# Last four softmax heads: values product with queries on partitions, sums divided on the copy, turns by VectorE in blocks

## The chip, the cores and the metric

The kernel runs on one core of one Trainium2 chip. The metric is the device time of one execution in microseconds; the time before is the median of three runs.

## The reference

One decoder layer on x of shape (1, 512, 2048), float32. What matters here is the dilated softmax mixer with eight heads of width 128:

```
h  = rms_norm(x, g1);  proj = h @ w_in            # all projections in one
qb, kb = rms_norm(qb), rms_norm(kb)               # per head
for (window, dilation) in ((128,1), (512,4), (2048,16)):
    logits = q @ k.T / sqrt(128) + bias[distance];  masked, causal
    o, lse = softmax(logits) @ v, log-sum-exp
out_b = sum over the three branches, weighted by softmax of their lse
x = x + concat(out_a, out_b) @ w_out              # out_a: gated linear attention, 4 heads
x = x + swiglu(rms_norm(x)) @ ...                 # w_gate, w_up, w_down
```

The kernel merges the three branches into one softmax over all 512 keys: a table holds, for each distance, the bias plus the logarithm of the number of branches in which the distance occurs.

## The kernel before

**Large products.** All five weight matrices are multiplied by a scheme with seven block products in place of eight (the names P1 to P7; `Pair` and `stream`). A step of the stream is one weight group of 256 rows by 512 columns. ScalarE casts it to a high part (`wh`, line 376), VectorE subtracts for the low part (`wl`, line 380), and sums of two weight blocks are made on VectorE too (line 294). TensorE then issues twelve matmuls of 128x512 (line 405), eight with `wh` and four with `wl`. Between the eight and the four, `p.step()` lets a piece of other work in. There are two buffers each of `wh` and `wl`.

**Other work.** The heads run as generators in the list `background`; one `yield` to the next is one piece, and a rate for each pair of weight blocks says how many pieces a step takes. The eight softmax heads come in twos: `dil_heads(h)` advances head h (lane 0) and h+1 (lane 1) in turn. Heads 0 to 3 start when the projection `vb0` is stored, heads 4 to 7 when `qb1` is. The latter run beside the pair of weight blocks that makes the output gate (28 steps, called the gate pair here). The three engines TensorE, ScalarE and VectorE and the queues follow an order that the framework's scheduler works out from the program; the order by hand in `PLAN` holds for the first pair alone.

**A softmax head.** It loads queries, keys, values and the bias table. For heads 0 to 3 (`s == 0`) the queries and keys are loaded by `load_blocks` (line 842): four DMAs per tile, one for each 32 columns, so that VectorE's transpose of 32x32 blocks (line 992) gives the full transpose. For heads 4 to 7 they are loaded by one DMA per tile (line 983) and turned by four TensorE transposes each (line 998) into a bank that ScalarE copies out, with the query gain (line 999). Then six pieces: scores of a query block (line 1007), bias and row extreme on VectorE (1010), exponential with row sum on ScalarE (1013), reciprocal (1016) and multiplication (1017) on VectorE; a piece later the turn of the weights on TensorE (1024) and their copy (1027); another piece later the product with the values, which stand as the stationary operand (1031), so that the output has the head's features on partitions, and its copy (1043). The last piece stores the head's output to `mix_d` (1047).

**After the heads.** `mix_d[4]` to `mix_d[7]` each hold two heads. The script `GATE` says at which step of the gate pair `mixed` does what: `T.g` loads the group's two halves of tokens (line 1222, two DMAs, as `kept[g, "t0"]` and `"t1"`), `A11.g`, `S3.g` and so on make sums of them (lines 1284 to 1294) and split them into high and low operands (lines 194 and 195). Groups 2 and 3 hold heads 4 to 7. The output projection (`w_out`) reads them.

All DMAs of this part are issued by SP, one after the other. A DMA whose data is not ready holds those behind it.

Of the kernel before, what the change touches and what calls it, by code (L numbers as in the profile page):

```python
# [10 lines left out]
F32 = mybir.dt.float32  # L11
F32R = mybir.dt.float32r
U32 = mybir.dt.uint32
AF = mybir.ActivationFunctionType
ALU = mybir.AluOpType
# [3 lines left out]
P = 128  # L19
S = 512  # L20
# [11 lines left out]
    13: "A11.1",  # L32
    14: "S3.1",
    16: "T.2",
    19: "A11.2",
    20: "S3.2",
    21: "2.0 S1.0",
# [1 line left out]
    23: "S1.1",  # L39
    24: "S2.0",  # L40
    25: "T.3 S2.1",
    27: "A11.3",
}
OUT = {
    0: "S3.3",
# [81 lines left out]
def block_kernel(ctx: ExitStack, tc: tile.TileContext, ins, out):  # L127
    nc = tc.nc
# [5 lines left out]
    apool = ctx.enter_context(tc.tile_pool(name="apool", bufs=28))  # L134
# [12 lines left out]
    def nm(s):  # L147
        uid[0] += 1
        return f"{s}_{uid[0]}"

    def dram(shape, name):
        return dr.tile(shape, F32, name=name, tag=name)

    def bank():
        return ps.tile([P, 512], F32, name=nm("bank"), tag="bank")

    def work(tag, shape=(P, 512), bufs=1):
        return mp.tile(list(shape), F32, name=nm(tag), tag=tag, bufs=bufs)

    def const(shape, name):  # L160
        return cp.tile(list(shape), F32, name=name, tag=name)
# [3 lines left out]
    load = nc.sync.dma_start  # L165
    store = nc.sync.dma_start

    mats = const([P, 2, P], "mats")
    ident, causal = (mats[:, i, :] for i in range(2))
# [11 lines left out]
    recent = {}  # L181
    done = set()
# [83 lines left out]
    def halves(t):  # L266
        return t.rearrange("p (b a) -> p b a", b=2)
# [377 lines left out]
    gq = const([P, 1], "gq")  # L645
# [78 lines left out]
    for g in range(4):  # L724
        for b in (2 * g, 2 * g + 1):
            if g < 2:
                t = apool.tile([P, 2, 512], F32, name=nm("xT"), tag="A")
# [57 lines left out]
    def gates():  # L785
# [30 lines left out]
        for h in range(4):  # L816
# [13 lines left out]
    proj = {n: dram([S, 512], n) for n in  # L830
            ("qa", "ka", "va0", "va1", "qb0", "kb0", "vb0", "vb1", "qb1", "kb1")}
    ong_d = [dram([2, P, 1024], f"ong_d{t}") for t in range(2)]
    mix_d = [dram([2, P, 2, 256], f"mix_d{b}") for b in range(8)]

    def head_cols(src, h, w=P):
        return src.rearrange("(t p) c -> p t c", p=P)[:, :, h * w : (h + 1) * w]

    def load_blocks(t, src, h):

        for a in range(4):  # L840
            c0 = h * P + 32 * a
            load(
                t[32 * a : 32 * a + 32, :].rearrange("i (c j) -> i c j", j=32),
                src[:, c0 : c0 + 32].rearrange("(c i) j -> i c j", i=32),
            )
# [115 lines left out]
    def dil_head(h, lane):  # L961


        s = h // 4

        def tile_(name):
            if lane == 0:
                return work("oT" if name == "o" else name)
            if name in "qk":
                return work(name + "T")  # L970
            return rpool.tile([P, 512], F32, name=nm("r"), tag="r")

        def logits(b):
            if lane == 0:
                return work("L", bufs=2)
            return tile_("L") if b % 2 else work("PT")

        qh, kh, vh = tile_("q"), tile_("k"), tile_("v").rearrange("p (t d) -> p t d", t=4)
        for dst, name in ((qh, f"qb{s}"), (kh, f"kb{s}")):
            if s == 0:  # L980
                load_blocks(dst, proj[name], h)
            else:
                load(dst.rearrange("p (t d) -> p t d", t=4), head_cols(proj[name], h % 4))
        load(vh, head_cols(proj[f"vb{s}"], h % 4))
        tb = tile_("T")
        load(tb, bass.AP(
            tensor=rep_d.tensor, offset=h * P * NB + P - 1, ap=[[NB - 1, P], [1, 512]]
        ))
        yield
        for src, g in ((qh, gq), (kh, 1.0)):  # L990
            if s == 0:
                nc.vector.transpose(src, src)
                if src is qh:
                    nc.scalar.activation(src, src, AF.Copy, scale=g)
                continue
            tp = bank()
            for t in range(4):
                nc.tensor.transpose(tp[:, t * P : (t + 1) * P], src[:, t * P : (t + 1) * P], ident)
            nc.scalar.activation(src, tp, AF.Copy, scale=g)
        yield  # L1000
        ot = tile_("o")
        lgs = {}

        def scores(b):
            n = P * (b + 1)
            lp = bank()
            nc.tensor.matmul(lp[:, :n], qh[:, b * P : (b + 1) * P], kh[:, :n], start=True, stop=True)  # L1007
            lg = lgs[b] = logits(b)
            st = work("mx", (P, 4), bufs=4)
            recent["head"] = nc.vector.tensor_tensor_reduce(  # L1010
                lg[:, :n], lp[:, :n], tb[:, 512 - n :], -1.0, 3.0e38, ALU.add, ALU.min, st[:, 0:1]
            ).ins
            nc.scalar.activation(
                lg[:, :n], lg[:, :n], AF.Exp, scale=-1.0, bias=st[:, 0:1], accum_out=st[:, 2:3]
            )
            nc.vector.reciprocal(st[:, 3:4], st[:, 2:3])
            recent["head"] = nc.vector.tensor_scalar(
                lg[:, :n], lg[:, :n], st[:, 3:4], None, op0=ALU.mult
            ).ins

        def turn(b, tp):
            n = P * (b + 1)
            for k in range(b + 1):
                nc.tensor.transpose(  # L1024
                    tp[:, k * P : (k + 1) * P], lgs[b][:, k * P : (k + 1) * P], ident
                )
            nc.scalar.copy(lgs[b][:, :n], tp[:, :n])

        def values(b, op):
            for k in range(b + 1):  # L1030
                nc.tensor.matmul(  # L1031
                    op, vh[:, k, :], lgs[b][:, k * P : (k + 1) * P], start=(k == 0), stop=(k == b)
                )

        for i in range(6):
            tp = bank() if 1 <= i <= 4 else None
            if i >= 2:
                op = tp[:, i * P : (i + 1) * P] if i < 4 else bank()[:, :P]
                values(i - 2, op)
            if tp is not None:  # L1040
                turn(i - 1, tp)
            if i >= 2:
                nc.scalar.copy(ot[:, (i - 2) * P : (i - 1) * P], op)
            if i < 4:
                scores(i)
            if i == 5:
                store(mix_d[4 + h // 2][:, :, h % 2, :].rearrange("b p n -> p b n"), halves(ot))
            yield

    def dil_heads(h):  # L1050

        lanes = [dil_head(h, 0), dil_head(h + 1, 1)]
        for _ in range(8):
            for lane in lanes:
                next(lane)
            if _ == 7:
                done.update((id(mix_d[4 + h // 2]), half) for half in range(2))
            yield
# [158 lines left out]
    def part(src, half):  # L1217
        def get(t=None):
            assert (id(src), half) in done
            if t is None:  # L1220
                t = rpool.tile([P, 2, 256], F32, name=nm("r"), tag="r")
            load(t, src[half])
            return t

        return get
# [32 lines left out]
    kept = {}  # L1258

    def scripted(pace, script):  # L1260

        k = [0]

        def go():
            pace()
            for word in script.get(k[0], "").split():
                mixed(*word.split("."))
            k[0] += 1

        return go  # L1270

    def mixed(name, g):
        g = int(g)
        tt = nc.vector.tensor_tensor
        if name == "T":
            t = apool.tile([P, 2, 2, 256], F32, name=nm("top"), tag="A")
            for i in range(2):
                kept[g, "t" + str(i)] = part(mix_d[4 + g], 1 - i)(t[:, i])
            return
        t0, t1 = kept[g, "t0"], kept[g, "t1"]  # L1280
        if name == "A11":
            opm.split(name, g, t0)
        elif name == "S3":
            tt(t1, t0, t1, op=ALU.subtract)
            opm.split(name, g, t1)
        elif name == "2":
            tt(t1, kept[g, "r1"], t1, op=ALU.subtract)
            tt(t0, t1, t0, op=ALU.add)
        elif name == "S1":
            opm.split(name, g, t0)  # L1290
        elif name == "S2":
            opm.split(name, g, t1)
        elif name == "S4":
            tt(t1, kept[g, "r0"], t1, op=ALU.subtract)
            opm.split(name, g, t1)
        else:
            opm.split(name, g, kept[g, "r0" if name == "A12" else "r1"])
# [402 lines left out]
```

## Time and profile before

| | |
|---|---|
| median of 3 runs | 1897.93 us |
| lowest, highest | 1895.16, 1898.85 us |
| the profiled execution | 1897.46 us, span 1895.70 us |
| TensorE busy | 1882.5 us, 99% |
| VectorE busy | 1691.9 us, 89% |
| ScalarE busy | 1073.1 us, 57% |
| DMA, mean | 182 GB/s |

In the rows PE is TensorE's matmul, PEld its weight load, DVE is VectorE, ACT ScalarE, SPq the queue of SyncE, which issues DMAs. L1007 is line 1007 of the kernel. `out<-in` names the program's tiles; `bank` is a PSUM bank, `wl` the low part of weights, `top` the tile of head outputs that `T.g` loads, `q`, `k`, `qT`, `kT` the queries and keys of lane 0 and lane 1.

### The profile page before, as it was taken

The numbers are of one execution on the slowest core, as the hardware profiler recorded it, in microseconds if no ns is written. First come the engines' busy times: TensorE is split into PE (matmuls) and PEld (weight loads), VectorE is DVE, ScalarE is ACT, GpSimd is POOL, SyncE is SP. The second block draws the span as 40 slices with busy tenths as digits, with TensorE's granted clock in tenths as the row PEclk, the third lists the DMA queues.
The fourth block names the chain that finished last, engine by engine and source line by source line (L and its number), as shares of the span: only waits on it lengthen the run. The fifth ranks groups of instructions, "written<-read, shape, count | busy, mean of one in ns | idle before, by whom it ended". The sixth has DMA issues, their size and how long they took to land.

```text
span 1895.7 us, 25155 instructions
## 1 busy us (share of the span) xinstructions
PE 1882.5 (99%) x8882; PEld 1636.0 (86%) x8882; DVE 1691.9 (89%) x1968; ACT 1073.1 (57%) x1583; POOL 4.5 (0%) x16
## 2 busy tenths in 40 slices
PE   9999999999999999999999999999999999999999
PEld 7888888888888888888888888888888888888887
DVE  8898898788899999888888888888889989999987
ACT  8664674577776675544544544544546546546543
POOL 0000000000000000000000000000000000000000
PEclk9999999999999999999999999999999999999999
DMA  9456545563628454465465465465466765785762
GB/s 341 161 151 237 174 154 156 173 220 107 206 101 270 146 195 143 119 185 185 130 184 178 121 196 161 123 200 155 135 200 202 207 231 184 264 279 186 241 222 67
DMA packets 271203, 345.46 MB, mean 182 GB/s; under 512 B 141908, under 2 KB 178685, under 8 KB 271078
## 3 DMA queue, kind: packets, MB, share of 16 engines
q1 hardware_dynamic: 270790, 343.73, 57.2%
q8 instruction: 69, 1.13, 0.2%
q14 instruction: 56, 0.46, 0.1%
q10 hardware_dynamic: 288, 0.14, 0.0%
HBM read 285.91 MB, written 60.32 MB: 183 GB/s over the span
## 4 chain that ended last, share of the span: by engine, by line
PE 86%; DVE 8%; DMA 3%; issue 2%; ACT 1%; SPq 0%; DVEq 0%; ACTq 0%
PE acc L405 79%; DVE wl L380 3%; PE acc L477 2%; DVE wa L294 2%; PE bank L1007 1%; PE bank L1031 1%; DMA xn_d<-oT 1%; PE bank L1024 0%; DVE AS L195 0%; PE bank L477 0%; PE bank L779 0%; DMA oT<-in_xt 0%; DMA x_d<-k 0%; DMA r<-xn_d 0%; DMA xT<-in_xt 0%
## 5 line engine op out<-in xcount | busy, mean ns | idle before, releaser
L405 PE MATMUL acc<-wh,AS 128*128 128x512 f32 x3008 | 711.3, 379 | 0.2 <-ACT wh L376 0.2
L405 PEld LDWEIGHTS acc<-wh,AS 128*128 128x128 f32 x3008 | 568.1, 189 | 82.7 <-ACT wh L376 2.3
L376 ACT CAST wh<-wa 128x1024 fp32r<-128x1024 f32 x376 | 393.7, 1048 | 391.7 <-PE acc L405 348.4
L405 PE MATMUL acc<-wh,AA 128*128 128x512 f32 x2256 | 533.4, 379 | 0.1
L380 DVE TENSOR_TENSOR wl<-wa,wh 128x1024 fp32r<-128x1024 f32 x376 | 456.6, 1216 | 81.7 <-ACT wh L376 74.8
L405 PEld LDWEIGHTS acc<-wh,AA 128*128 128x128 f32 x2256 | 426.2, 189 | 60.9 <-ACT wh L376 0.5
L405 PE MATMUL acc<-wl,AS 128*128 128x512 f32 x1504 | 392.7, 383 | 3.7 <-DVE wl L380 3.6
L405 PEld LDWEIGHTS acc<-wl,AS 128*128 128x128 f32 x1504 | 282.0, 189 | 49.4 <-DVE wl L380 8.6
L405 PE MATMUL acc<-wl,AA 128*128 128x512 f32 x1128 | 292.8, 382 | 0.2 <-DVE wl L380 0.2
L405 PEld LDWEIGHTS acc<-wl,AA 128*128 128x128 f32 x1128 | 211.9, 189 | 31.3 <-issue 1.0
L376 ACT CAST wh<-wb 128x1024 fp32r<-128x1024 f32 x94 | 98.5, 1048 | 124.7 <-PE acc L405 122.7
L376 ACT CAST wh<-wc 128x1024 fp32r<-128x1024 f32 x94 | 98.5, 1048 | 112.6 <-PE acc L405 106.7
L376 ACT CAST wh<-wd 128x1024 fp32r<-128x1024 f32 x94 | 98.6, 1049 | 92.2 <-PE acc L405 90.8
L380 DVE TENSOR_TENSOR wl<-wd,wh 128x1024 fp32r<-128x1024 f32 x94 | 114.8, 1221 | 24.2 <-ACT wh L376 24.0
L380 DVE TENSOR_TENSOR wl<-wb,wh 128x1024 fp32r<-128x1024 f32 x94 | 114.6, 1219 | 16.8 <-ACT wh L376 14.5
L380 DVE TENSOR_TENSOR wl<-wc,wh 128x1024 fp32r<-128x1024 f32 x94 | 114.4, 1217 | 7.4 <-ACT wh L376 4.6
L294 DVE TENSOR_TENSOR wb<-wd,wb 128x1024 f32<-128x1024 f32 x94 | 114.2, 1217 | 0.0
L294 DVE TENSOR_TENSOR wa<-wc,wa 128x1024 f32<-128x1024 f32 x94 | 113.9, 1216 | 0.0
L294 DVE TENSOR_TENSOR wa<-wb,wa 128x1024 f32<-128x1024 f32 x94 | 113.6, 1210 | 0.3
L294 DVE TENSOR_TENSOR wa<-wd,wa 128x1024 f32<-128x1024 f32 x94 | 113.4, 1217 | 0.4
L339 DVE SCALAR_TENSOR_TENSOR seed<-acc,rs,seed 128x512 f32<-128x512 f32 x96 | 71.5, 746 | 21.2 <-PE acc L405 21.2
L320 ACT ACTIVATE seed<-acc,rs 128x512 f32<-128x512 f32 x96 | 60.4, 679 | 0.5 <-PE acc L405 0.5
(326 smaller groups left out, 1243.3 us busy)
## 6 DMA issues: line engine op xcount, KB each, us to landing
wa<-in_w_gate SPq DMA_DIRECT2D x44, 512.0 KB, 4.5
wb<-in_w_up SPq DMA_DIRECT2D x44, 512.0 KB, 4.2
wd<-in_w_up SPq DMA_DIRECT2D x44, 512.0 KB, 4.4
wc<-in_w_gate SPq DMA_DIRECT2D x44, 512.0 KB, 3.4
wa<-in_w_in SPq DMA_DIRECT2D x24, 512.0 KB, 4.5
wc<-in_w_in SPq DMA_DIRECT2D x24, 512.0 KB, 4.0
wb<-in_w_in SPq DMA_DIRECT2D x24, 512.0 KB, 5.9
wd<-in_w_in SPq DMA_DIRECT2D x24, 512.0 KB, 5.8
```

The source lines that it names most:

```text
L294: nc.vector.tensor_tensor(src, other, src, op=ALU.subtract)
L320: nc.scalar.activation(halves(t), unfolded(src[m]), AF.Copy, scale=self.scale(half, m))
L339: nc.vector.scalar_tensor_tensor(halves(seed[m]), unfolded(src[m]), self.scale(half, m), halves(seed[m]), op0=ALU.mult, op1=ALU.add,)
L376: nc.scalar.copy(high[k], sources[k])
L380: made[k] = recent["low"] = nc.vector.tensor_tensor(low[k], sources.pop(k), high[k].bitcast(F32), op=ALU.subtract).ins
L405: nc.tensor.matmul(p.dst[prod][m], a[:, jj, hl, m * P : (m + 1) * P], folded(w[i][:, jj, :]), start=fresh and g == 0 and i == 0 and jj == ...
L477: recent["pe"] = nc.tensor.matmul(dst[name][m], a[:, jj, hl, m * P : (m + 1) * P], folded(w[:, jj, :]), start=(name, m) not in opened, sto ...
L1007: nc.tensor.matmul(lp[:, :n], qh[:, b * P : (b + 1) * P], kh[:, :n], start=True, stop=True)
L1031: nc.tensor.matmul(op, vh[:, k, :], lgs[b][:, k * P : (k + 1) * P], start=(k == 0), stop=(k == b))
```

## The change

Heads 4 to 7 (`s` is 1) are done otherwise in five points. Their queries and keys are loaded with `load_blocks` and turned by VectorE, as those of heads 0 to 3; the gain of the queries is applied by ScalarE in place. The values product has its operands exchanged: the turned weights are stationary and the values move, so the output has queries on partitions. Since a row sum then belongs to a partition, the multiplication by the reciprocal on VectorE is left out, and the output's copy on ScalarE takes the reciprocal as its scale. The outputs are stored with tokens as rows (`mix_d[6]` and `mix_d[7]` are now 512 by 256). `T.2` and `T.3` load them with `load_blocks`, eight DMAs each, and a new word `V.g` in the script turns the tile by two VectorE transposes, two steps after `T.g`. For heads 0 to 3 the output's copy is an activation with the scale 1.0 instead of a plain copy, and the small tile of row statistics has six buffers instead of four.

```diff
@@ GATE
     16: "T.2",
+    18: "V.2",
     19: "A11.2",
...
-    27: "A11.3",
+    27: "V.3 A11.3",
@@
-    mix_d = [dram([2, P, 2, 256], f"mix_d{b}") for b in range(8)]
+    mix_d = [dram([2, P, 2, 256], f"mix_d{b}") for b in range(6)]
+    mix_d += [dram([S, 256], f"mix_d{b}") for b in (6, 7)]
@@ dil_head
         for dst, name in ((qh, f"qb{s}"), (kh, f"kb{s}")):
-            if s == 0:
-                load_blocks(dst, proj[name], h)
-            else:
-                load(dst.rearrange("p (t d) -> p t d", t=4), head_cols(proj[name], h % 4))
+            load_blocks(dst, proj[name], h % 4)
...
-        for src, g in ((qh, gq), (kh, 1.0)):
-            if s == 0:
-                nc.vector.transpose(src, src)
-                if src is qh:
-                    nc.scalar.activation(src, src, AF.Copy, scale=g)
-                continue
-            tp = bank()
-            for t in range(4):
-                nc.tensor.transpose(tp[:, t * P : (t + 1) * P], src[:, t * P : (t + 1) * P], ident)
-            nc.scalar.activation(src, tp, AF.Copy, scale=g)
+        for src in (qh, kh):
+            nc.vector.transpose(src, src)
+        nc.scalar.activation(qh, qh, AF.Copy, scale=gq)
...
             nc.vector.reciprocal(st[:, 3:4], st[:, 2:3])
-            recent["head"] = nc.vector.tensor_scalar(
-                lg[:, :n], lg[:, :n], st[:, 3:4], None, op0=ALU.mult
-            ).ins
+            if s == 0:
+                recent["head"] = nc.vector.tensor_scalar(
+                    lg[:, :n], lg[:, :n], st[:, 3:4], None, op0=ALU.mult
+                ).ins
@@ values
-                nc.tensor.matmul(
-                    op, vh[:, k, :], lgs[b][:, k * P : (k + 1) * P], start=(k == 0), stop=(k == b)
-                )
+                v, p = vh[:, k, :], lgs[b][:, k * P : (k + 1) * P]
+                if s:
+                    v, p = p, v
+                nc.tensor.matmul(op, v, p, start=(k == 0), stop=(k == b))
...
-                nc.scalar.copy(ot[:, (i - 2) * P : (i - 1) * P], op)
+                scale = sums[i - 2][:, 3:4] if s else 1.0
+                nc.scalar.activation(ot[:, (i - 2) * P : (i - 1) * P], op, AF.Copy, scale=scale)
...
-            if i == 5:
+            if i == 5 and s:
+                store(
+                    head_cols(mix_d[4 + h // 2], h % 2), ot.rearrange("p (t d) -> p t d", t=4)
+                )
+            elif i == 5:
@@ mixed
         if name == "T":
+            if g >= 2:
+                t = apool.tile([P, 2, 512], F32, name=nm("top"), tag="A")
...
+                for h in range(2):
+                    load_blocks(t[:, h, :], mix_d[4 + g], h)
+                for i in range(2):
+                    kept[g, "t" + str(i)] = t[:, :, 256 * (1 - i) : 256 * (1 - i) + 256]
+                return
...
+        if name == "V":
+            t = kept[g, "whole"]
+            for h in range(2):
+                nc.vector.transpose(t[:, h, :], t[:, h, :])
             return
```

## Rows read from the trace of the kernel before

**Rows 1.** The page's first part: busy us (share) x instructions.

```profile
PE 1882.5 (99%) x8882; PEld 1636.0 (86%) x8882; DVE 1691.9 (89%) x1968; ACT 1073.1 (57%) x1583; POOL 4.5 (0%) x16
```

**Rows 2.** Windows: us, then PE, PEld, DVE, ACT, POOL busy, clock, DMA share, GB/s.

```profile
482.60:496.00 13.40, 12.55 (x69) 10.90 (x69) 8.97 (x19) 9.40 (x18) 0.00 (x0) 1.00 0.96 325
496.00:513.00 17.00, 17.00 (x97) 14.30 (x98) 15.31 (x38) 14.30 (x35) 0.00 (x0) 1.00 0.32 109
513.00:554.00 41.00, 39.58 (x203) 33.95 (x202) 40.48 (x50) 31.13 (x51) 0.00 (x0) 1.00 0.41 142
```

**Rows 3.** The chain that ended last, from 451 us: start, us, what.

```profile
451.25 1.89 PE bank L998 x16
...
482.91 4.17 DMA mix_d<-r
...
487.50 4.47 DMA top<-mix_d
...
512.66 0.60 DVE seed L1202
...
553.78 2.86 PE acc L405 x12
```

**Rows 4.** Timeline, second group of turns; below it line 1031, duration min/median/max.

```profile
487.60 0.60 PE L998 MATMUL bank<-mats,q 128*128 128x128 f32 x4
...
489.27 1.11 PE L405 MATMUL acc<-wl,AS 128*128 128x512 f32 x4
...
L1031 PE MATMUL bank<-L,v x80: 272/275/275, 347.8 to 520.3; 128*128 128x128 f32 x80
```

**Rows 5.** Transposes of line 992: duration min/median/max, first and last start.

```profile
L992 DVE STREAM_TRANSPOSE kT<-kT x2: 701/702/704, 307.0 to 386.8; 128x512 f32<-128x512 f32 x2
...
L992 DVE STREAM_TRANSPOSE qT<-qT x2: 704/704/705, 333.1 to 380.4; 128x512 f32<-128x512 f32 x2
```

**Rows 6.** Timeline of VectorE and TensorE, 453 to 459 us.

```profile
453.19 0.68 DVE L195 TENSOR_TENSOR AA<-top,AA 128x512 fp32r<-128x512 f32 x1
...
455.60 1.21 DVE L380 TENSOR_TENSOR wl<-wa,wh 128x1024 fp32r<-128x1024 f32 x1
...
458.52 0.68 PE L405 MATMUL acc<-wl,AS 128*128 128x512 f32 x2
```

**Rows 7.** Timeline, 492 to 498 us; in brackets idle time before and its end.

```profile
492.00 0.69 DVE L1284 TENSOR_TENSOR top<-top 128x512 f32<-128x512 f32 x1 [2.40 <-DMA top<-mix_d]
...
492.61 1.22 DVE L380 TENSOR_TENSOR wl<-wb,wh 128x1024 fp32r<-128x1024 f32 x1
...
495.99 0.30 PE L1024 MATMUL bank<-mats,L 128*128 128x128 f32 x1 [0.85 <-DVE L L1017]
...
496.92 1.21 PE L405 MATMUL acc<-wl,AS 128*128 128x512 f32 x4
```

**Rows 8.** ScalarE's copies of line 999: duration min/median/max.

```profile
L999 ACT ACTIVATE q<-bank,gq x2: 671/678/685, 452.2 to 488.8; 128x512 f32<-128x512 f32 x2
L999 ACT ACTIVATE k<-bank x2: 582/583/584, 452.8 to 489.3; 128x512 f32<-128x512 f32 x2
```

**Rows 9.** VectorE's multiplications of line 1017, lane 0: duration min/median/max.

```profile
L1017 DVE TENSOR_SCALAR L<-L,mx x16: 285/380/482, 338.8 to 510.0; 128x128 f32<-128x128 f32 x4, 128x256 f32<-128x256 f32 x4, 128x384 f32<-128x384 f32 x4, 128x512 f32<-128x512 f32 x4
```

**Rows 10.** Block loads of line 842 and, last, the operand load at 487 us.

```profile
L842 SPq DMA_DIRECT2D q<-qb x8: 326/480/538, 312.4 to 358.4; - x8
...
DMA to landing us min/median/max: 2.0/2.4/4.1
...
487.13 0.80 SPq L1222 DMA_DIRECT2D top<-mix_d  x2
```

**Rows 11.** Window of block loads of the first heads, columns as in rows 2.

```profile
356.90:364.50 7.60, 7.60 (x43) 6.48 (x42) 6.66 (x13) 3.95 (x9) 0.00 (x0) 1.00 0.67 121
```

**Rows 12.** Timeline, second operand tile of these heads, loads and first use.

```profile
527.92 0.80 SPq L1222 DMA_DIRECT2D top<-mix_d  x2
...
532.55 0.68 DVE L1284 TENSOR_TENSOR top<-top 128x512 f32<-128x512 f32 x1
```

More of the change, by code (lines that the diff above doesn't have):

```diff
@@ L989, in dil_head @@
         yield
-        for src, g in ((qh, gq), (kh, 1.0)):
-            if s == 0:
-                nc.vector.transpose(src, src)
-                if src is qh:
-                    nc.scalar.activation(src, src, AF.Copy, scale=g)
-                continue
-            tp = bank()
-            for t in range(4):
-                nc.tensor.transpose(tp[:, t * P : (t + 1) * P], src[:, t * P : (t + 1) * P], ident)
-            nc.scalar.activation(src, tp, AF.Copy, scale=g)
+        for src in (qh, kh):
+            nc.vector.transpose(src, src)
+        nc.scalar.activation(qh, qh, AF.Copy, scale=gq)
         yield
         ot = tile_("o")
-        lgs = {}
+        lgs, sums = {}, {}
         def scores(b):
@@ L1008, in scores @@
             lg = lgs[b] = logits(b)
-            st = work("mx", (P, 4), bufs=4)
+            st = sums[b] = work("mx", (P, 4), bufs=6)
             recent["head"] = nc.vector.tensor_tensor_reduce(
@@ L1275, in mixed @@
         if name == "T":
+            if g >= 2:
+                t = apool.tile([P, 2, 512], F32, name=nm("top"), tag="A")
+                kept[g, "whole"] = t
+                assert (id(mix_d[4 + g]), 1) in done
+                for h in range(2):
[3 more added lines that the diff above has]
+                return
             t = apool.tile([P, 2, 2, 256], F32, name=nm("top"), tag="A")
@@ L1278, in mixed @@
                 kept[g, "t" + str(i)] = part(mix_d[4 + g], 1 - i)(t[:, i])
+            return
+        if name == "V":
+            t = kept[g, "whole"]
+            for h in range(2):
+                nc.vector.transpose(t[:, h, :], t[:, h, :])
             return
```

## The prediction

> **What bounds the kernel now.** I read the page's busy shares first [rows 1]: TensorE is at 99%, VectorE at 89%, ScalarE at 57%. With TensorE so near to full, a microsecond of matrix work counts unless another engine is late at that place, so the stretches around the change come next [rows 2]. From 482.6 to 496 us TensorE is idle for 0.85 us, and VectorE works for 8.97 of 13.40. From 496 to 513 TensorE is full. From 513 to 554 VectorE has 40.48 of 41.00 us and TensorE 39.58, so it is idle for 1.42. The granted clock is 1.00 throughout, so the clock is no part of the argument.
>
> The chain of waits says the same by place [rows 3]. The sixteen turns of queries and keys of heads 4 and 5, at 451.25, lie on it, and TensorE holds it until the last output of these heads. There it leaves TensorE: the output is stored (4.17 us) and loaded as the operand tile (4.47 us), and VectorE goes on from 492.00; TensorE takes it up again at 495.99 [rows 7]. From 512.66 the chain is mostly VectorE, with short pieces of ScalarE and TensorE, until 553.78, where TensorE has it again. So what the change takes from TensorE ahead of 482.6 is worth its full length, what it adds on VectorE after 513 costs almost its full length, and between 482.6 and 496 the transfers decide.
>
> **The change part by part.** The sum is made against the profiled execution, 1897.46 us (span 1895.70, 1.76 around it). The median of the three runs is 0.47 us higher, well inside their spread of 3.69; I apply the difference to the median.
>
> *Turns that leave TensorE.* Each of the four heads turned queries and keys in eight 128x128 pieces: 32, in two groups. The first holds the chain for 1.89 us [rows 3]; the second goes from 487.60 to the next weight matmul at 489.27, 1.67 us [rows 4]. Together -3.56 us. The values products keep their count, 40, and their 128 columns, with the operands exchanged. One is 272 to 275 ns before [rows 4]. With the operands exchanged the trace has none; its other products of this size are turns, at 0.118 us apiece on the chain (1.89 over 16), so between -0.1 and +0.1 us for each; I take 0, since neither the count nor the columns change, and keep 40 times 0.02, 0.8 us, for the range.
>
> *Query and key turns on VectorE.* Eight transposes of 128x512 come in, about 0.70 us each in the first four heads [rows 5]; pieces of that size start 0.60 apart back to back, as the four from 453.19 to 455.60 do [rows 6]. One key tile of the first heads was turned at 307.0, 26 us before the first query tile of its lane at 333.1 [rows 5]: the order puts them into gaps when they are loaded early. I therefore place the keys of heads 4 and 5 in gaps, and all four turns of heads 6 and 7 in the 4.43 us that VectorE idles from 482.6 to 496 [rows 2]. The two queries of heads 4 and 5 come late. At that place the low part made from 455.60 to 456.81 is used at 458.52, a lead of 1.7 us [rows 6]. With TensorE 1.89 us sooner the lead is gone, and 1.3 us of turning makes it 1.5 late; with the keys there too it is 2.8. If the four pieces from 453.19, operands that are wanted later, go behind (2.4 us), nothing is lost. Bounds 0 and +2.8; I take +0.8, half of the case with only the queries in place.
>
> *Queries scaled in place on ScalarE.* Before, a query tile's scaled copy was 0.68 us and a key tile's plain copy 0.58 [rows 8]; the second goes, the first stays. ScalarE loses work and idles 43% of the time: 0. But a scaling that waits for its turn holds the cast queued behind it on ScalarE, and TensorE waits for that cast; this is one more way to the +2.8.
>
> *Multiplications that leave VectorE, the scale on ScalarE's copy.* Sixteen go, 0.285 to 0.482 us by size [rows 9]: four times the median 0.38 is 1.52 per head, 6.1 in all, against twelve transposes of 0.60 to 0.70, 7.2 to 8.4. VectorE gains 1 to 2 us of work. The multiplications also stood between the exponential and the turn of the weights: the 0.85 us at 495.99 ended at one [rows 7]. I take half of it, -0.4; the bounds are -0.85 and 0. A copy with a scale costs up to 0.10 us more per 512 columns than a plain one [rows 8]; for the 32 output copies, a quarter as wide, that is under 3.2 us even at the full 0.10, on the engine that idles: 0.
>
> *Loads in blocks.* Each query or key tile becomes four DMAs instead of one, 24 more; each of the two operand tiles eight instead of two, 12 more. SP takes 0.33 to 0.54 us for one, 0.48 the median [rows 10], so 17 us more of SP. The twelve extra ones of heads 6 and 7, 5.8 us, are queued ahead of three things: these heads' values and bias, weight loads, and the head store at 482.91 [rows 3]. I let that store go out when it did, not 1.89 us sooner. The operand load waits for the store as before, then issues for 3.84 us instead of 0.80, and the new turns stand behind it. Block loads land in 2.0 to 4.1 us [rows 10]: 487.13 + 3.84 + 3.5 = 494.5, against 492.00 before, and two turns end at 495.7. If VectorE's next low part stands behind that, it begins 3.1 us later than at 492.61; it had a lead of 496.92 - 493.83 = 3.1 us [rows 7], but TensorE now comes 3.56 sooner. That is +3.6, and +5 if the last block is slow. If the low part stands ahead of the turns, nothing is lost, because the step asks for the turned tile only three steps later. Bounds 0 and +5; I take +0.8, nearer to the lower end, since VectorE has 4.43 us of idle time there to put things right.
>
> The Trainium skill, in "DMA: Bandwidth & Descriptors", section "Specifications", asks for pieces of at least 512 B for full rate. The blocks move rows of 32 floats, 128 B. The trace agrees: around the first heads' block loads the engines move 121 GB/s at a share of 0.67 [rows 11], and 325 at 0.96 from 482.6 on [rows 2], which is 181 against 339 at full share. By this rule the upper price of the operand load, +5, would stand in the sum: +2.4 in all, 1900.3.
>
> *Turning the second operand tile.* Two transposes, 1.2 us, land in the stretch that VectorE fills. Their loads are issued from 527.92 for 3.84 and land near 535; the tile was first used at 532.55 [rows 12]. The multiplications of heads 6 and 7 that go before 513 (3.0 us) give VectorE a lead, of which TensorE can use only its own 1.42 us of idle time [rows 2]. Bounds -1.4 and +3.5 (1.2, and a wait of 2.3); I take +0.6, half of the turning.
>
> Sum: -3.56 + 0.8 - 0.4 + 0.8 + 0.6 = -1.8 us, so 1896.1.
>
> **The rivals.** First, all of it is hidden: the turns fall into gaps, and the waits of 0.85 and 1.42 us go as well. That is -3.56 - 2.27 = -5.8, so 1892.1. For it: the first four heads load in blocks and turn on VectorE with TensorE at 7.60 of 7.60 us [rows 11]. Against it: VectorE had 6.66 of 7.60 there and is full after 513.
>
> Second, slower: VectorE stands at the turn of the first operand tile until its eight block loads have landed, with a low part of the weights queued behind, and TensorE stands too. It decides once the last block lands after about 493. Its price is the +5, with my values elsewhere +2.4, 1900.3; with the upper prices at the queries (+2.8) and the second tile (+3.5) too, and no gain on the multiplication, +7.7, 1905.7. For it: VectorE already idled 2.40 us on this load with two DMAs [rows 7]. Against it: the lead of 3.1 us. The skill's rule above speaks for this rival.
>
> Third, the change does not reach the time: VectorE's run from 492.00 to 553.78 starts with the operand load, so what TensorE saves is given back as idle time. Then VectorE's balance there decides: 3.0 off, 2.4 on, and some later landing, about -0.1: 1897.8. For it the chain; against it that TensorE idles only 1.42 us there, so it cannot be far behind.
>
> **How the numbers follow.** A difference of 0.2%, 3.8 us, is about what a measurement of this kernel can tell from none. Forecast, -1.8: 0.46. All hidden: 0.28. Slower: 0.18, of which 0.02 stay under 0.2%. Not reaching: 0.08. Faster takes the hidden case and 0.02 of the forecast's tail, 0.30; slower 0.16; within 0.2% 0.54. The range begins at 1890.5, beyond the hidden case by the 0.8 us kept for the products and 0.8 more for the runs, and ends at 1902.5, which leaves out only the part of the slower case with most upper prices at once.
>
> **What would show it.** Right: no TensorE turns near 451 and 487, and VectorE idle for under 3 us on the operand load. Wrong: TensorE idle by more than 1.5 us at 450 to 460 (queries), more than 2 from 480 to 500 (first tile), or more than 2.5 from 513 to 554 (second tile); or another order of the work ahead of 400 us, where only the output copies change.

## The result, and the profile after

The changed kernel takes 1908.30 us (median of six runs, 1905.64 to 1911.03), against 1897.35 for the kernel before on the same chip: ratio 1.0059, interval 1.0049 to 1.0069. It is slower by 11 us where a gain of 1.8 was forecast, and lies outside the range. The profiled execution took 1908.11 us with a span of 1906.3.

The page's first part, as in [rows 1]:

```profile
PE 1884.1 (99%) x8850; PEld 1634.7 (86%) x8850; DVE 1695.6 (89%) x1964; ACT 1073.4 (56%) x1579; POOL 4.4 (0%) x16
```

TensorE has 32 instructions fewer and is busy 1.6 us longer. An engine that does less in more time ran slower somewhere, and the windows say where. These are the stretches of [rows 2] in the changed kernel, and below them two narrower ones:

```profile
450.00:460.00 10.00, 9.21 (x44) 7.77 (x43) 9.77 (x13) 5.55 (x7) 0.00 (x0) 1.00 0.46 99
482.60:496.00 13.40, 13.40 (x64) 11.56 (x62) 10.12 (x16) 7.10 (x12) 0.00 (x0) 1.00 0.95 207
496.00:513.00 17.00, 11.85 (x67) 7.82 (x66) 9.43 (x29) 10.67 (x32) 0.00 (x0) 1.00 0.79 304
513.00:554.00 41.00, 38.44 (x182) 33.15 (x183) 38.95 (x50) 30.35 (x48) 0.00 (x0) 0.92 0.50 155
...
495.00:515.50 20.50, 12.88 (x73) 8.52 (x71) 12.53 (x35) 13.05 (x35) 0.00 (x0) 0.98 0.69 260
515.50:521.00 5.50, 5.50 (x13) 4.41 (x14) 5.50 (x8) 5.19 (x9) 0.00 (x0) 0.50 0.24 74
```

The stretch 482.6 to 496, in which I put the danger, is full (13.40 of 13.40). The next, where TensorE had 17.00 of 17.00, has 11.85, and no other engine is full in it either: VectorE 9.43, ScalarE 10.67. Three engines that all idle for 30% or more at once point to pieces that wait for one another. From 495 to 515.5 TensorE idles 20.50 - 12.88 = 7.62 us, and behind that its granted clock is 0.50, the lower of the two levels (1.2 GHz).

To place the loss I set the two traces side by side by the weight steps: TensorE multiplies each weight tile in a fixed order, and the start of a step's low-part matmuls (`wl`, line 406, before 405) is easy to find in both. Start in us, and how far the changed kernel is behind:

```
step   before    after   behind
 10    448.50   448.72    +0.22
 12    455.57   453.90    -1.67   first group of turns gone
 16    472.84   472.37    -0.47   most of it given back
 20    489.27   487.13    -2.14   second group gone
 22    496.92   492.54    -4.38
 23    502.47   495.13    -7.34
 24    508.22   519.05   +10.83
 26    516.01   525.38    +9.37
 31    532.83   542.02    +9.19
 75    655.59   666.72   +11.13   and about so to the end
```

At step 20 and again at step 26 both kernels have done the same pieces of the heads, so the loss is what lies between these: 9.37 + 2.14 = 11.5 us. (That it reads -7.34 at step 23 is no gain: pieces that had stood ahead of that step stand behind it now.) Before step 20 the change was worth -2.14; after step 26 the difference stays between +8.7 and +11.6.

TensorE's timeline between steps 23 and 24, changed kernel (start, us, engine, line, what, in brackets idle time before and its end):

```profile
493.83 1.46 PE L406 MATMUL acc<-wh,AS 128*128 128x512 f32 x6
495.13 1.03 PE L406 MATMUL acc<-wl,AS 128*128 128x512 f32 x4
498.21 0.46 PE L999 MATMUL bank<-kT,qT 128*128 128x128 f32 x2 [2.06 <-issue]
...
504.55 0.71 PE L1027 MATMUL bank<-v,L 128*128 128x128 f32 x4 [0.66 <-ACT r L1038]
...
511.05 0.60 PE L1017 MATMUL bank<-mats,r 128*128 128x128 f32 x4
515.48 3.78 PE L406 MATMUL acc<-wh,AA 128*128 128x512 f32 x8 [3.83 <-ACT wh L377]
519.05 1.91 PE L406 MATMUL acc<-wl,AA 128*128 128x512 f32 x4
520.76 2.19 PE L406 MATMUL acc<-wh,AA 128*128 128x512 f32 x8
522.79 1.03 PE L406 MATMUL acc<-wl,AA 128*128 128x512 f32 x4
```

Between the four at 495.13 and those at 515.48 there is no weight matmul. Before, the products of heads 6 and 7 lay between those of five weight steps (2, 4, 16, 12, 14 of them to a step), and TensorE did weights while ScalarE and VectorE prepared the next piece. Now 47 of them stand in one step. (Counted are products of the program: a score or a values product is two instructions in the rows, a turn is one. The 16 and the 47 hold eight turns of other work, line 1155 before and 1154 now.) Of the 7.62 us of idle time 2.06 lie ahead of the first of them, 1.7 between them, where a product waits for the exponential, the turn's copy or the output copy, and 3.83 at the end, where TensorE waits for a cast. ScalarE in the same stretch shows why:

```profile
512.68 0.62 ACT L195 CAST AA<-top 128x512 fp32r<-128x512 f32 x1
513.86 0.62 ACT L195 CAST AS<-top 128x512 fp32r<-128x512 f32 x1 [0.56 <-DVE top L1297]
514.38 1.04 ACT L377 CAST wh<-wc 128x1024 fp32r<-128x1024 f32 x1
```

The cast of the weights is queued behind the splits of the operand tile, and these behind VectorE, whose two turns of that tile stand among its own pieces of the heads:

```profile
494.83 0.70 DVE L990 STREAM_TRANSPOSE qT<-qT 128x512 f32<-128x512 f32 x1
...
497.30 0.70 DVE L990 STREAM_TRANSPOSE kT<-kT 128x512 f32<-128x512 f32 x1
...
504.49 0.69 DVE L1291 STREAM_TRANSPOSE top<-top 128x512 f32<-128x512 f32 x1
...
511.94 0.70 DVE L1291 STREAM_TRANSPOSE top<-top 128x512 f32<-128x512 f32 x1
```

The order is another on SP too, whose queue goes in order. The DMAs around the store of heads 4 and 5, first in the changed kernel, then before (start and us on SP's queue):

```profile
471.38 2.40 SPq L844 DMA_DIRECT2D q<-qb  x4
473.83 1.55 SPq L844 DMA_DIRECT2D k<-kb  x3
481.71 0.38 SPq L1042 DMA_DIRECT2D mix_d<-oT  x1
...
483.00 0.55 SPq L844 DMA_DIRECT2D k<-kb  x1
...
484.78 2.02 SPq L844 DMA_DIRECT2D qT<-qb  x4
486.84 2.13 SPq L844 DMA_DIRECT2D kT<-kb  x4
...
490.10 4.20 SPq L844 DMA_DIRECT2D top<-mix_d  x8
494.93 2.11 SPq L256 DMA_DIRECT2D wc<-in_w_in  x4
```

```profile
473.62 0.36 SPq L983 DMA_DIRECT2D qT<-qb  x1
474.03 0.51 SPq L983 DMA_DIRECT2D kT<-kb  x1
477.54 2.59 SPq L255 DMA_DIRECT2D wc<-in_w_in  x3
482.19 0.46 SPq L1047 DMA_DIRECT2D mix_d<-oT  x1
```

Before, the queries and keys of heads 6 and 7 and three of the four loads of wc went out ahead of the store at 482.19. Now the fourth block of the first head's keys is caught behind the store, which waits for outputs of heads 4 and 5, and with it everything queued after: head 7's queries go out at 484.78 instead of 473.62, wc at 494.93 instead of 477.54, 17.4 us later. The order of the three engines is worked out from the program ahead of the run, and I take it that the scheduler put the pieces of heads 6 and 7 where it reckoned their late inputs to come; the trace does not show its reckoning. What it shows is that the data was there sooner: head 7's keys were issued by 488.97 and landed 2.0 to 2.1 us after their issue, some 6 us ahead of VectorE's turn at 497.30, and from 489.92 to 515.48 the chain that ended last goes through no DMA. The time is lost by the order of the pieces, not by waiting for a load.

### The profile page after: what moved, and what is told of

Read it like the earlier page. It is cut to its first block, busy times and chain, and to the rows that moved or that the text cites. A ratio compares the mean times of both kernels' runs of the same rounds, so it can differ in the third digit from the quotient of the medians.

```text
span 1906.3 us, 25147 instructions
## 1 busy us (share of the span) xinstructions
PE 1884.1 (99%) x8850; PEld 1634.7 (86%) x8850; DVE 1695.6 (89%) x1964; ACT 1073.4 (56%) x1579; POOL 4.4 (0%) x16
## 4 chain that ended last, share of the span: by engine, by line
PE 88%; DVE 6%; DMA 3%; issue 2%; ACT 1%; SPq 0%; DVEq 0%; ACTq 0%
PE acc L406 82%; PE acc L478 2%; DVE wl L381 2%; DVE wa L295 1%; PE bank L1027 1%; PE bank L999 1%; DMA xT<-in_xt 1%; PE bank L1017 0%; PE bank L478 0%; PE bank L780 0%; DMA x<-in_x 0%; DMA wa<-in_w_in 0%; DMA wa<-in_w_gate 0%; DMA xn_d<-oT 0%; DVE AS L196 0%
```

## The experiments

My theory: the blocks cost their time on SP's queue, and the late loads bunch the heads into one weight step, where the order's cover is gone. Rivals: VectorE's turns themselves; the exchanged values product or the copy with a scale; the number and small rows of the DMAs as such. Ratios are to the kernel before, with their intervals.

**One half of the change alone.** The values product, the scale on the copy and the operand tiles in blocks, with queries and keys as before:

```diff
-            load_blocks(dst, proj[name], h % 4)
+            if s == 0:
+                load_blocks(dst, proj[name], h)
+            else:
+                load(dst.rearrange("p (t d) -> p t d", t=4), head_cols(proj[name], h % 4))
...      (and TensorE's turns of these tiles as before)
```

> The changed kernel with queries and keys of heads 4 to 7 loaded by one DMA and turned by TensorE as before; the exchanged values product, the scale on the copy and the turned operand tiles stay. Queue theory: the heads run between the weight steps again, 1894 to 1900 us; the operand tiles' 12 extra DMAs cost at most 2. VectorE theory with the first operand tile as the culprit: 1901 to 1906 us.

Measured 1894.75 us, 0.9994 (0.9985 to 1.0003). The values product and the scale are cleared: TensorE is full from 490 to 520,

```profile
490.00:520.00 30.00, 30.00 (x174) 26.03 (x173) 27.59 (x53) 26.66 (x60) 0.00 (x0) 1.00 0.55 182
```

and the heads lie over the weight steps as they did before.

The other half, the kernel before with query and key blocks and VectorE's turns:

```diff
-            if s == 0:
-                load_blocks(dst, proj[name], h)
-            else:
-                load(dst.rearrange("p (t d) -> p t d", t=4), head_cols(proj[name], h % 4))
+            load_blocks(dst, proj[name], h % 4)
...
+        for src in (qh, kh):
+            nc.vector.transpose(src, src)
+        nc.scalar.activation(qh, qh, AF.Copy, scale=gq)
```

> The kernel before with only the queries and keys of heads 4 to 7 loaded in blocks on SP's queue and turned by VectorE; values product, multiplications and operand tiles as before. Queue theory: the second lane's tile is late again, 1903 to 1910 us. Theory that the operand tiles or the exchanged product cost the time: 1893 to 1898 us.

Measured 1898.03 us, 1.0014 (1.0005 to 1.0024): a miss. The query and key blocks alone don't make the 11 us. They make part of it: wc goes out at 491.26, 33 products (counted as above) stand between steps 23 and 24, and from step 20 to step 26 the kernel goes from 2.19 ahead to 0.82 behind. These 3.0 us are about what the turns had saved. So two parts that each cost little cost much together, and I crossed them.

**Blocks of the heads times blocks of the operand tiles.** In rows means one DMA per query or key tile, and two per operand tile; VectorE's turns stay in all three. All three compute something else for heads 4 to 7 and serve for the time alone.

```diff
-            load_blocks(dst, proj[name], h % 4)
+            if s == 0:
+                load_blocks(dst, proj[name], h)
+            else:
+                load(dst.rearrange("p (t d) -> p t d", t=4), head_cols(proj[name], h % 4))
```

> The changed kernel, but queries and keys of heads 4 to 7 are loaded in rows by one DMA per tile (24 DMAs fewer on SP) and VectorE still turns them in 32x32 blocks. What it computes for these heads is then not attention on the right queries; the work on the engines is that of the changed kernel. Queue theory (the block loads on SP make the second lane's tile late, and the heads' pieces stand together between two weight steps): 1892 to 1898 us, TensorE idle for under 3 us from 490 to 520. VectorE theory (the turns, or the low parts behind them, cost the time): 1903 to 1910 us.

```diff
-                    load_blocks(t[:, h, :], mix_d[4 + g], h)
+                    load(
+                        t[:, h, :].rearrange("p (t d) -> p t d", t=4), head_cols(mix_d[4 + g], h)
+                    )
```

> The changed kernel, but the two operand tiles of heads 4 to 7 are loaded in rows, two DMAs each instead of eight (12 fewer on SP), and still turned by VectorE. The output projection then reads these heads' outputs in the wrong places. Queue theory: the weight loads go out some 3 us sooner and one more weight step stands between the heads' pieces, 1896 to 1901 us, near the kernel with the query and key turns alone. VectorE theory: 1904 to 1909 us.

The third has both edits:

> Both of these together: no block loads beyond those of the kernel before, all twelve turns on VectorE. Its heads 4 to 7 are not the right ones for the same two reasons. Queue theory: 1891 to 1896 us, the 3.56 us of TensorE's turns saved and at most 2 given back. VectorE theory: 1902 to 1909 us.

```
                        tiles in blocks                   tiles in rows
heads in blocks   1908.30, 1.0059 (1.0049-1.0069)   1897.63, 1.0009 (0.9999-1.0019)
heads in rows     1893.20, 0.9987 (0.9977-0.9996)   1895.50, 0.9997 (0.9988-1.0007)
```

The three were measured beside other runs of the kernel before than the changed kernel was, so the ratios are compared. By them the blocks of the operand tiles cost nothing where the heads' loads are short (0.10% less), and 0.50%, 9.5 us, where they are long; the blocks of the heads cost 0.12%, 2.3 us, without those of the tiles and 0.72%, 13.7 us, with them. With heads in rows and everything else as changed, the kernel is 0.13% faster than before. In its trace it goes from 1.33 behind at step 10 to 3.71 ahead at step 26; these 5.0 us are the 3.56 of the turns, 1.05 of a wait (below), and 0.4 more. With tiles in rows it goes from 1.97 ahead at step 20 to 0.98 behind at step 26, the 3.0 us of the half change again. VectorE's turns, the values product and the copy with a scale therefore cost nothing that shows where the heads' loads are short. The windows of the same 30 us, first heads in rows, then tiles in rows, then the changed kernel:

```profile
490.00:520.00 30.00, 30.00 (x172) 26.02 (x171) 27.93 (x54) 25.84 (x58) 0.00 (x0) 1.00 0.57 177
```

```profile
490.00:520.00 30.00, 27.60 (x141) 22.59 (x140) 26.77 (x54) 24.10 (x54) 0.00 (x0) 0.94 0.74 260
```

```profile
490.00:520.00 30.00, 22.38 (x106) 16.49 (x106) 20.71 (x47) 21.73 (x51) 0.00 (x0) 0.91 0.64 214
```

Idle 0, 2.4 and 7.6 us, with 16, 33 and 47 products in the fullest step; in the last two the granted clock is below 1.00 too (0.94 and 0.91).

**Which two heads.** Blocks and VectorE's turns for heads 6 and 7 only, then for 4 and 5 only, the other two as before:

```diff
-            load_blocks(dst, proj[name], h % 4)
+            if h < 4 or h >= 6:     # the second kernel: if h < 6
+                load_blocks(dst, proj[name], h % 4)
+            else:
+                load(dst.rearrange("p (t d) -> p t d", t=4), head_cols(proj[name], h % 4))
...      (and the turns by the same condition)
```

> The changed kernel with block loads and VectorE turns for queries and keys of heads 6 and 7 alone; those of heads 4 and 5 are loaded by one DMA and turned by TensorE as before. Queue theory: the loads of heads 6 and 7 are the ones that stand around the head stores and ahead of the weight loads, so the loss stays, 1904 to 1909 us. Theory that every block load costs alike: half of the loss, 1899 to 1903 us.

> The reverse: block loads and VectorE turns for heads 4 and 5, one DMA and TensorE's turns for heads 6 and 7. Queue theory: SP is not crowded when heads 4 and 5 load, so no loss, 1893 to 1897 us. Theory that every block load costs alike: 1899 to 1903 us.

Measured 1.0054 (1.0041 to 1.0067), 1906.57 us (12.6 us lost from step 20 to 26), and 0.9994 (0.9985 to 1.0003), 1894.67 us. All of the loss comes from the two heads whose loads go out next to the store and the operand tile. With heads 6 and 7 in blocks SP shows the same late weights and TensorE the same 47:

```profile
484.52 2.02 SPq L844 DMA_DIRECT2D qT<-qb  x4
...
495.56 2.02 SPq L256 DMA_DIRECT2D wc<-in_w_in  x4
```

With only 4 and 5 in blocks head 7's queries go out at 474.21 and wc at 475.71, and the heads stay spread:

```profile
474.21 0.36 SPq L985 DMA_DIRECT2D qT<-qb  x1
475.71 5.80 SPq L256 DMA_DIRECT2D wc<-in_w_in  x4
```

**The weights asked for sooner.** If wc alone were late, asking for these weights three steps sooner should mend it:

```diff
+            if self.hold and prod == "P7":
+                self.quarter("c", g)
```

> The changed kernel, but the four weight loads of the product P2 in the gate pair are asked for three steps sooner, ahead of the loads of heads 6 and 7 and of the operand tile. Weights theory (the weight loads at 494.9 instead of 477.5 are what stops the weight steps): 1894 to 1899 us. Queue theory in the form that the late queries and keys of the second lane stop the heads, and the heads then stand together: still 1902 to 1910 us.

Measured 1901.17 us, 1.0026 (1.0016 to 1.0037), between the two expectations. The first of wc now goes out at 475.97, and some 6 of the 11 us come back. But only two of the four loads of wc go out early; the others go at 492.26 and 499.26. Head 7's queries still go out at 486.87, and 40 products stand together, two steps later. So asking sooner mends about half, and the run does not part the late weights from the late heads.

**The operand tile later.** Its load and turns four to five steps further on, away from the heads' loads:

```diff
-    16: "T.2",
-    18: "V.2",
...
+    20: "T.2",
...
+    23: "V.2 S1.1",
```

> The changed kernel with the first operand tile of these heads loaded four steps later in the script (20 instead of 16, its turn and its splits after it), so that its eight block loads come behind the weight loads of P2. Queue theory: as with that tile loaded in rows, 1895 to 1900 us. Theory that the block loads of heads 6 and 7 do the whole damage by themselves: 1904 to 1909 us.

Measured 1902.99 us, 1.0037 (1.0024 to 1.0050), again between. 33 stand together instead of 47 and 7.6 us are lost instead of 11.5. TensorE waits 3.26 us ahead of the first of them, at 499.09. The profile puts that wait down to wc, but the product reads head 7's keys, which VectorE turns from 498.18 to 498.88; which of the two held it stays open. As many products in one step cost 3.0 us in the half change, so their number alone is not the price.

**Another queue.** The 32 block loads of these heads on ScalarE's queue instead of SP's:

```diff
-            load_blocks(dst, proj[name], h % 4)
+            load_blocks(dst, proj[name], h % 4, nc.scalar.dma_start if s else load)
...      (load_blocks takes the function that issues)
```

> The changed kernel, but the 32 block loads of queries and keys of heads 4 to 7 are issued from ScalarE's queue instead of SP's. Queue theory (the added DMAs on SP push the second lane's queries and keys behind the head stores and the weight loads behind those, and the heads' pieces then stand together between two weight steps): 1893 to 1899 us, TensorE idle under 3 us from 490 to 520, no fall of the clock. VectorE theory (the turns themselves are late or hold the low parts, whichever queue loads them): 1904 to 1910 us, as the changed kernel.

Measured 1907.20 us, 1.0057 (1.0040 to 1.0074): a miss for the theory as I had stated it. The bunch is gone (0, 2, 4, 16, 12, 14 to a step, as before), yet the loss is there, all of it from step 20 to 21 (+0.11 to +11.82). It has another cause, in the same views:

```profile
491.92 2.47 ACTq L844 DMA_DIRECT2D qT<-qb  x4
494.54 2.12 ACTq L844 DMA_DIRECT2D kT<-kb  x4
496.75 1.04 ACT L377 CAST wh<-wb 128x1024 fp32r<-128x1024 f32 x1 [11.68 <-DMA kT<-kb]
497.85 3.39 PE L406 MATMUL acc<-wh,AS 128*128 128x512 f32 x8 [7.45 <-ACT wh L377]
...
503.90 0.56 PE L999 MATMUL bank<-kT,qT 128*128 128x128 f32 x2 [2.44 <-DVE kT L990]
...
490.00:520.00 30.00, 20.12 (x90) 16.19 (x89) 17.98 (x39) 17.94 (x39) 0.00 (x0) 0.83 0.59 157
```

ScalarE computes nothing for 11.68 us while its block loads stand at the head of its queue, the cast behind them waits, and TensorE for the cast 7.45 us. It waits another 2.44 us for VectorE's turn of head 7's keys, and the clock, which the theory had at no fall, stands at 0.83 on the mean from 490 to 520 (last line, a window). The queue that held SP's loads now holds ScalarE's work. The Trainium skill, in "DMA: Bandwidth & Descriptors", section "Rules for kernel authors", says that spreading DMAs over engines only saves issue time. That saving was what this kernel was after, and the trace shows it paid for with 11.68 us of the other engine.

**The DMAs alone.** The kernel before, its TensorE turns kept, with each query and key tile of these heads loaded by four DMAs of 32 columns:

```diff
-                load(dst.rearrange("p (t d) -> p t d", t=4), head_cols(proj[name], h % 4))
+                for a in range(4):
+                    c = slice(32 * a, 32 * a + 32)
+                    load(
+                        dst.rearrange("p (t d) -> p t d", t=4)[:, :, c],
+                        head_cols(proj[name], h % 4)[:, :, c],
+                    )
```

> The kernel before, with each query and key tile of heads 4 to 7 loaded by four DMAs of 32 columns (24 more on SP, the same 128 B pieces as the block loads), turned by TensorE as before. Theory that the DMAs cost by themselves (SP's time and small pieces): 1900 to 1906 us. Theory that they cost only through the order of the work that follows from them, which stays here as it was before: 1895 to 1899 us.

Measured 1899.38 us, 1.0018 (1.0008 to 1.0027). The order of the heads is that of before, but for the first group of turns, which falls into two steps. So the further DMAs cost about 0.18% by themselves, of the 0.59% of the whole change. In the trace it is 1.36 us behind at step 10, where these heads have not begun, 2.68 at step 12 and 3.44 at step 22: some 2.1 us belong to the loads. The rest of the loss needs the bunch. SP is no emptier here than in the half change, and its loads are late too:

```profile
479.38 2.02 SPq L985 DMA_DIRECT2D qT<-qb  x4
...
484.25 0.44 SPq L255 DMA_DIRECT2D wc<-in_w_in  x1
...
491.65 1.88 SPq L255 DMA_DIRECT2D wc<-in_w_in  x2
```

Head 7's queries go out 5.8 us later than before and the first of wc 6.7, and yet nothing bunches. Nor does it with VectorE's turns and loads in rows. Heads 6 and 7 stood together only in the six kernels in which their block loads on SP and VectorE's turns of them meet; neither the number of the DMAs nor a delay of some 6 us does it by itself. Why the scheduler orders the two together so was not tested: no run held the order fixed.

Of the versions that leave nothing of the computation out, the best two, 0.9994 each, have intervals that hold 1. The query and key blocks on GpSimd's queue were not tried.

## Why the prediction was wrong, by its steps

*Turns that leave TensorE:* right. Line 998 of before has no successor, and with the heads in rows all of it comes through. In the changed kernel the second group's 1.67 came (from -0.47 to -2.14), while 1.2 of the first's 1.89 were given back by step 16, where 25 products of heads 4 and 5 stand in one step. The values product with operands exchanged was the 0 that I took (first line; the second belongs to the next step):

```profile
L1027 PE MATMUL bank<-v,L x40: 273/275/377, 467.2 to 529.6; 128*128 128x128 f32 x40
...
L990 DVE STREAM_TRANSPOSE qT<-qT x4: 703/704/706, 333.4 to 494.8; 128x512 f32<-128x512 f32 x4
```

*Query and key turns on VectorE:* 0.70 us each, as said, and hidden where the heads' loads are in rows; I had priced them at +0.8. In the changed kernel three of them lie on the chain that ended last (at 457.66, 463.51 and 494.91, 2.0 us). From 450 to 460 TensorE idles 0.79 us, under the 1.5 that I had set as a sign.

*Multiplications and the scale:* the 0.85 us at 495.99 [rows 7] is gone where the product alone is changed (1.05 us gained at step 22, against 0.4 in the sum). The copy with a scale took the whole 0.10 us that I had as its bound, and at 128 columns; only sixteen of my 32 copies have a scale per row:

```profile
L1038 ACT ACTIVATE oT<-bank x8: 255/271/282, 349.5 to 425.3; 128x128 f32<-128x128 f32 x8
L1038 ACT ACTIVATE oT<-bank,mx x8: 347/371/390, 468.9 to 530.1; 128x128 f32<-128x128 f32 x8
```

For sixteen copies that is 1.6 us of ScalarE, and hidden (1073.4 us busy against 1073.1).

*Loads in blocks:* this is the step that failed. It counted the 36 DMAs and their time on SP about rightly (four took 2.02 to 2.40 us, eight 4.20), and named what the twelve of heads 6 and 7 are queued ahead of: their values and bias, weight loads, and the store. Then it priced the operand tile alone, +0.8 and at most +5. The other entries in that list, and the order that came of them, carried the loss. It also took the store to stand behind the loads, while the order put it among them: one block caught behind a store that waits for outputs held up head 7 and the weights for 11 to 17 us. And it kept the order of TensorE as it was; the new order, with heads 6 and 7 in one step, is what lost the time. The clock, which I left out because it was 1.00 before, is a part of it. Measured, the place is +11.5 us: 6.8 more of TensorE idle (7.62 against 0.85), some 3.1 of half clock behind it (1.89 for the eight `wh` matmuls that took 3.78, 0.88 for the four of `wl`, 0.30 for the next eight), and 1.6 that I did not separate.

The operand tile, on which the slower rival rested, was not late by its DMAs: its first turn at 504.49 waited for none of them, ten microseconds after the last was issued. My sign for it, TensorE idle for more than 2 us from 480 to 500, did come (2.43), but 2.06 of that lie at 498.21, ahead of a product of head 7's keys. The Trainium skill's "DMA: Bandwidth & Descriptors", section "Specifications", has rows under 512 B below full rate, and the trace agrees: from 482.6 to 496, where blocks of head 7 and of the tile go out, the engines move 207 GB/s at a share of 0.95, 218 at full share, against 339 before. By that rule the rival would have given 1900.3. Slow blocks are thus seen, but they were not what TensorE waited for: the rival had the sign, in the right 30 us, for the wrong reason.

*Turning the second operand tile:* TensorE idles 41.00 - 38.44 = 2.56 us from 513 to 554, just over the 2.5 that I had set. But 2.48 of it lie ahead of 515.48, in the wait for the cast, and from step 26 to step 31 nothing is lost (+9.37, +9.19). The step's +0.6 was not needed.

## What to carry to other kernels

When one DMA becomes four on an in-order queue, list everything queued behind them, a store that waits for results above all, and price each entry, the weights and the next inputs too, before the tile that the change is about. Where a scheduler works out the order, a change of loads can move work out of its cover, and that can cost more than the load's own lateness; compare the order of the pieces first. See how many dependent pieces stand together in one step: of heads 6 and 7, 16 cost nothing, 33 cost 3.0 us twice and 7.6 once, 47 cost 11.5 and 12.6; of heads 4 and 5, 25 and 36 each cost 1.2. The number is a warning and not a price. A busy engine that does fewer instructions in more busy time is a sign to look at its clock.

## What the runs showed of the hardware

TensorE's granted clock, 1.00 throughout before, stood at 0.50 for 6.83 us (514.5 to 521.4). TensorE had idled 7.6 of 20.5 us, and without a break from 511.65; weight matmuls ran when it rose. Eight matmuls of 128x512 took 3.78 us, which at full clock take 1.89 as here:

```profile
523.65 1.89 PE L406 MATMUL acc<-wh,AA 128*128 128x512 f32 x8
```

The sum of idle time does not tell whether it falls. In the kernel of the second half alone TensorE idled 3.28 of 30 us and it did not:

```profile
490.00:520.00 30.00, 26.72 (x145) 21.97 (x144) 27.19 (x60) 23.98 (x55) 0.00 (x0) 1.00 0.70 258
```

With the operand tiles in rows TensorE idled 2.40 us in the same stretch, and the clock stood at 0.50 for 3.4 us (the window above, 0.94).

With the block loads on its queue ScalarE did no arithmetic for 11.68 us, and a copy of 128x128 out of a matmul bank with a scale per row takes 0.37 us against 0.27 without.
